# One inference step of a gated recurrent layer: the FFN's fourth input pair as seven block products, and a moved split, cast and key page in branch A

## The chip, the core and the metric

The kernel runs on one core of a Trainium2 chip. The metric is the device time of the whole program in microseconds (us), here the median of three runs. Engines are called as the profile calls them: PE is TensorE, DVE VectorE, ACT ScalarE, POOL GpSimd, SP SyncE, which only issues DMAs here.

## What is computed

One layer of a decoder on 520 tokens (512 of a prompt, 8 of a sample group), with D = 1024 and an inner FFN width of 2816. The arithmetic that the change touches, cut from the reference:

```python
z = h @ w_in                                 # xr, gr, q, k, v, fl, ga, gb are columns of z
xc, conv_new = causal_dwconv(xr, conv_buf, conv_w, conv_b)
hr, h_last = rg_lru(xc, h0, pos0, rg_wr, rg_br, rg_wi, rg_bi, rg_lambda)
ya = (hr * gelu(gr)) @ w_proj_a              # branch A
yb = attend(q, k, v, logf).reshape(B, T, ATTN_W) @ w_proj_b
mixed = (sigmoid(ga) * ya + sigmoid(gb) * yb) @ w_o
x = x + g1 * mixed
h2 = rms_norm(x, norm2_g) * (1.0 + sc2) + sh2
gu, up = split(h2 @ w_ffn_in, 2)
x = x + g2 * ((silu(gu) * up) @ w_ffn_out)
```

The sample group's attention also runs over its cache: 64 pages of keys and 64 of values, 512 KB each.

## The kernel before

**Products.** Everything is kept with features on the partitions and the 520 tokens on the free axis, in two halves of 260 (`L_` and `R_` in the FFN). Each operand of a large product is held as a rounded part and the rest (names ending in h and l for activations, `whi` and `wlo` for weights, both halves of `wb` for a block), and each product of a 128x128 weight block with 260 tokens is three matmuls: rounded by rounded, rest of the weight by rounded, rounded by rest of the activation. `product` makes a 128-feature output: eight k blocks by three matmuls by two halves, 48 matmuls into two PSUM banks. Products are counted by `state["n"]`. Numbers 0 to 31 are the input projections of branch A and the gates (xr, gr, ga, gb), 32 is k0, 33 v0, 34 to 41 are pa0 to pa7, the products with `w_proj_a`; then come the rest of attention, pb, wo and the FFN.

**Weights.** SP fetches chunks of 1024x256 (`wraw`, two buffers; chunks of w_fo go into the pool of page buffers `pg`). `split_upto(n)` makes every unit up to number n ready: ScalarE casts (`whi`, line 250), VectorE subtracts (`wlo`, line 252). A chunk's buffer comes free when its last unit is split. `split` does the same for activations (lines 346 and 347).

**Branch A.** `lru_gates` makes the recurrence's gates by small matmuls and sigmoids, then `lru_exp`, `lru_root`, `lru_scan`; `lru_mul` multiplies the state by the gelu, and `lru_g` splits that into the operand `g` of the pa products (`gh`, `gl`). In the last round of the loop (i = 6) the order is written out: behind the gates of 6, with `issue_after`, come `both(lru_mul, 4)`, `both(lru_g, 4)` and the split of the weights of two products ahead; then ga6, the gates of 7, ga7. A ga product's two banks are evacuated by ScalarE (`tA`, line 1194).

**Cache pages.** At each of the products 0 to 41 `tick` fetches as many pages of keys as the table `KEYS` says, from GpSimd's queue, multiplies them with the queries on VectorE and sums; `VALUES` names the products that also fetch pages of values. Small matmuls `pv` take these up.

**FFN.** The inner width is 22 pairs of 128 (gate and up). Pairs 0 and 1 (`PLAIN`) are made together, the left half of the tokens first, while the right half of h2 is still being normalised (banks fi0 to fi3). Pairs 2 and 3 (below `GROUP`) are two plain products each, `fig` and `fiu`. From pair 4 on `fast_tile` makes a pair with seven block products in Strassen's manner (Winograd's form) instead of eight: the two 128-feature outputs and the two k halves are the 2x2 blocks of the weights, the two k halves and the two token halves those of the input. The products A11, S2, S3, S1, A12, A22, S4 have four k blocks each, 12 matmuls, and go into the banks X, Y, W, Z (fi4x, fi4y and so on). Names are those of the weight's block: A11, A12 and A22 are blocks of it, S1 to S4 sums that GpSimd makes in `split_block` (`ws`, line 265). The input's sums are `u` and `w` (four tiles each, one of each for k and k + 4), which `h2_blocks` makes once on GpSimd, four instructions of 128x260 for each k, and which `split_blocks` splits into `tuh`, `tul`, `twh`, `twl`. S2 and S3 take w's halves; S1 and A22 take u's; A11, A12 and S4 take h2 itself. `JOIN` puts two products of the FFN's second matrix (`fo`) behind S2 and A12 of a pair.

**What sets the order.** Tile's scheduler orders the instructions on each engine from their order in the code, a simulated run and the priorities; `issue_after` adds an order and no data. `defer(k, fn)` runs fn at the end of the k-th product from now. `h2_blocks` stands before pair 2 in the code, and `split_blocks` behind the first and the second of the next products.

Of the kernel before, what the change touches and what calls it, by code (L numbers as in the profile page):

```python
# [67 lines left out]
def kernel(ctx, tc, xT, par1, par, gates, b_f, cst, cse, own, cache_k, cache_v, cache_lf, pt,  # L68
# [75 lines left out]
    GROUP = 4  # L144
    PLAIN = 2
    LAST = 16
    JOIN = {}
# [15 lines left out]
    for jt in range(FF // 128):  # L163
        c = len(chunks)
        chunks.append(cols(w_fi, 128 * jt, 128) + cols(w_fi, FF + 128 * jt, 128))
        if jt < GROUP:
            whole(c)
            continue
        for name in BLOCKS:
            units.append((c, name, 4))  # L170
            if name in JOIN[jt]:
                g, i = JOIN[jt][name]
                if i % 2 == 0:
                    joined.add(len(chunks))
                    chunks.append(cols(w_fo, 128 * i, 256, 128 * GROUP * g, GROUP))
                units.append((max(joined), 128 * (i % 2), GROUP))
# [17 lines left out]
    def flush():  # L194
        while stores:
# [4 lines left out]
    KEYS = dict(zip(range(42), (2, 2, 0, 0, 1, 2, 2, 2, 1, 1, 1, 1, 2, 2, 2, 1, 0, 1, 0, 1, 2, 2, 2, 2, 1, 1, 1, 1, 2, 2, 1, 2,  # L200
                                1, 1, 1, 2, 1, 1, 1, 1, 2, 0)))
    VALUES = (19, 21, 22, 25, 28, 29, 31, 35, 37, 39)
# [56 lines left out]
    def split_block(raw, name):  # L259
        if name == "A11":  # L260
# [3 lines left out]
            blocks.update(A11=a11, A12=a12, A22=a22, S1=s1, S2=s2, S3=s3, S4=s4)  # L264
            pool.tensor_tensor(s1, a21, a22, ALU.add)  # L265
            pool.tensor_tensor(s2, s1, a11, ALU.subtract)
            pool.tensor_tensor(s3, a11, a21, ALU.subtract)
            pool.tensor_tensor(s4, a12, s2, ALU.subtract)
# [325 lines left out]
    m = None  # L594
# [606 lines left out]
    for i in range(0, KT, 2):  # L1201
# [35 lines left out]
        else:  # L1237
            lru_gates(i)
            with tc.issue_after(state["gate"].ins):
                both(lru_mul, i - 2)  # L1240
                both(lru_g, i - 2)
                split_upto(state["n"] + 2)
            gate_a(i)
            lru_gates(i + 1)
            gate_a(i + 1)
# [516 lines left out]
    L_, R_ = slice(0, HALF), slice(HALF, NT)  # L1762
    tb, traw = [], {}

    def h2_blocks(k):
        b1, b2 = h2raw[k], h2raw[k + 4]
        u, w = slot("u"), slot("w")
        with tc.issue_after(state["blocks"].ins) if k != 3 else nullcontext():
            first = pool.tensor_tensor(w[:, R_], b2[:, R_], b1[:, R_], ALU.subtract)
        if k == 3:  # L1770
            state["blocks"] = first
        with tc.issue_after(state["blocks"].ins):
            pool.tensor_tensor(u[:, L_], b1[:, R_], b1[:, L_], ALU.subtract)
            pool.tensor_tensor(w[:, L_], b2[:, R_], u[:, L_], ALU.subtract)
            pool.tensor_tensor(u[:, R_], b2[:, L_], w[:, L_], ALU.subtract)
        traw[k] = u, w

    def split_blocks(k0):
        with tc.issue_after(state["silu"].ins):
            for k in range(k0, k0 + 2):  # L1780
                u, w = traw[k]
                tb.append((split("tu", u), split("tw", w)))

# [5 lines left out]
    def fast_tile(jt, ac):  # L1789
# [9 lines left out]
        for m_, name in enumerate(BLOCKS):  # L1799
# [24 lines left out]
            run_later(n)  # L1824
            if name in JOIN[jt]:
                g, i = JOIN[jt][name]
# [5 lines left out]
    for j in range(2):  # L1832
        for m in range(2 * PLAIN):
# [7 lines left out]
            if j or m:  # L1841
                with tc.issue_after(state["root"].ins):
                    for fn, *args in ready:
                        fn(*args)
                ready.clear()
            first = u + 2 * PLAIN
            if j == 0:
                load_chunks(units[first + m][0])
            elif m:
                split_upto(first + m - 1)  # L1850
    for t in ts:
# [3 lines left out]
    for jt in range(PLAIN, FF // 128):  # L1855
        if jt == PLAIN:
            for k in (3, 0, 1, 2):
                h2_blocks(k)
            defer(0, lambda: split_blocks(0))
            defer(1, lambda: split_blocks(2))  # L1860
        ac.append(fast_tile(jt, ac) if jt >= GROUP else ffn_tile(jt))
    last_product(ac[LAST:])

# [63 lines left out]
```

## Time and profile before

| | before |
|---|---|
| median of 3 runs | 1000.09 us |
| lowest, highest | 999.8, 1001.43 us |
| profiled execution, its span | 1000.87 us, 999.1 us |
| instructions | 21582 |
| TensorE (PE) | 8156 matmuls |
| VectorE (DVE) | 774.9 us busy, 1386 instructions |
| ScalarE (ACT) | 553.1 us busy, 1131 instructions |
| GpSimd (POOL) | 357.9 us busy, 444 instructions |
| DMA | 204.03 MB, 204 GB/s over the span |

The span runs from the first to the last instruction that is counted as work; the time of the execution lies 1.77 us above it. Rows of a timeline give the start and the duration of an instruction in us from the start of the span, its engine, line, operation, output and inputs with shapes, and in square brackets how long the engine had stood idle and what released it. SPq and POOLq are queues of DMA issues. Rows of waits give the idle time of one group of instructions in all, its count, and the longest. Rows of windows give the stretch and its length, and for each engine the busy time and the count (PE, PEld, DVE, ACT, POOL), then the granted clock, the DMA share and the rate in GB/s.

### The profile page before, as it was taken

What the parts mean: (1) busy time and instruction counts of PE and PEld (TensorE: products, weight loads), DVE (VectorE), ACT (ScalarE), POOL (GpSimd) and SP (SyncE); (2) the same over time, 40 slices, a digit from 0 to 9 for tenths busy, and PEclk for the clock granted to TensorE, in tenths of its full rate; (3) what the DMA queues carried; (4) which work ended last, traced back from release to release, by engine and by line L of the source; (5) the groups of instructions that cost most, each with busy time, mean ns of one, the idle gap of its engine ahead of it and who ended that gap; (6) DMA issues with size and microseconds to landing.
All of it is one profiled execution on the core that took longest, in us unless ns stands there. A gap on an engine that the chain in (4) does not pass through costs nothing.

```text
span 999.1 us, 21582 instructions
## 1 busy us (share of the span) xinstructions
PE 981.7 (98%) x8156; PEld 912.6 (91%) x8156; DVE 774.9 (78%) x1386; ACT 553.1 (55%) x1131; POOL 357.9 (36%) x444
## 2 busy tenths in 40 slices
PE   7999999999999999999999999999999999999996
PEld 5889999999898988888888879999999999999996
DVE  5599899979899877876664445879888887888764
ACT  5435669766941576777762224544444444445453
POOL 0254142523354166545300003394334242434112
PEclk9999999999999999999999999999999999999998
DMA  9989756887979998897778994142424334133112
GB/s 320 335 282 325 224 169 185 262 288 243 307 235 365 324 287 274 286 294 200 256 265 290 341 338 130 45 127 64 128 64 127 97 94 121 49 106 107 64 64 86
DMA packets 164506, 204.03 MB, mean 204 GB/s; under 512 B 9635, under 2 KB 128051, under 8 KB 164339
## 3 DMA queue, kind: packets, MB, share of 16 engines
q1 hardware_dynamic: 148162, 151.14, 47.9%
q0 software_dynamic: 12560, 45.10, 13.6%
q10 hardware_dynamic: 3680, 6.42, 1.7%
q8 instruction: 64, 1.05, 0.5%
q14 instruction: 40, 0.32, 0.1%
HBM read 189.54 MB, written 13.09 MB: 203 GB/s over the span
## 4 chain that ended last, share of the span: by engine, by line
PE 87%; ACT 4%; DVE 4%; DMA 2%; issue 1%; SPq 0%; POOL 0%; POOLq 0%; DVEq 0%; ACTq 0%
PE fo L311 13%; PE wo L311 5%; PE pb L311 4%; PE gb L311 4%; PE v L311 4%; PE k L311 4%; PE ga L311 3%; PE xr L311 3%; PE pa L311 3%; PE pv L946 3%; PE gr L311 2%; PE po L1416 2%; PE sc L1353 2%; PE ptt L1382 2%; PE ada L378 2%; PE fi L311 1%
## 5 line engine op out<-in xcount | busy, mean ns | idle before, releaser
L250 ACT CAST whi<-wraw 128x1024 fp32r<-128x1024 f32 (+1 forms) x79 | 82.1, 1040 | 92.2 <-PE pb L311 34.3
L252 DVE TENSOR_TENSOR wlo<-wraw,whi 128x1024 fp32r<-128x1024 f32 (+1 forms) x79 | 97.8, 1238 | 24.4 <-ACT whi L250 22.3
L274 ACT CAST wb<-ws 128x512 fp32r<-128x512 f32 x72 | 44.8, 622 | 88.4 <-PE fo L311 61.2
L311 PE MATMUL fo<-ach,wb 128*128 128x260 f32 x512 | 93.4, 283 | 0.0
L275 DVE TENSOR_TENSOR wb<-wraw,wb 128x512 fp32r<-128x512 f32 x86 | 76.0, 883 | 5.3 <-ACT wb L274 4.3
L311 PEld LDWEIGHTS fo<-ach,wb 128*128 128x128 f32 x512 | 78.9, 188 | 0.0
L265 POOL TENSOR_TENSOR ws<-wraw 128x512 f32<-128x512 f32 x18 | 24.4, 1355 | 151.8 <-DMA wraw<-in_w_fi_dram 86.3
L274 ACT CAST wb<-wraw 128x512 fp32r<-128x512 f32 x86 | 53.5, 622 | 35.8 <-ACT cp L1814 6.2
L311 PE MATMUL fo<-acl,wb 128*128 128x260 f32 x256 | 72.3, 282 | 0.0
L275 DVE TENSOR_TENSOR wb<-ws,wb 128x512 fp32r<-128x512 f32 x72 | 60.8, 845 | 14.2 <-ACT wb L274 12.5
L794 POOL DMA_DIRECT2D pg<-in_cache_k_dram x70 | 37.7, 539 | 92.0 <-DVE S L858 47.3
L857 DVE TENSOR_TENSOR pg<-pg,qb 128x1024 f32<-128x1024 f32 x48 | 57.9, 1220 | 2.2 <-DMA pg<-in_cache_k_dram 2.1
L858 DVE TENSOR_REDUCE S<-pg 128x16 f32<-128x1024 f32 x48 | 57.3, 1208 | 0.3
L1373 POOL TENSOR_SCALAR p<-p,mu 128x128 f32<-128x128 f32 (+3 forms) x28 | 34.5, 1243 | 53.8 <-DVE mu L1369 40.5
L311 PEld LDWEIGHTS fo<-acl,wb 128*128 128x128 f32 x256 | 48.3, 189 | 0.0
L1367 ACT ACTIVATE p<-p,mu 128x128 f32<-128x128 f32 (+3 forms) x64 | 35.4, 555 | 17.3 <-DVE mu L1366 16.8
L407 POOL TENSOR_TENSOR ss<-ss,sq 128x260 f32<-128x260 f32 x10 | 7.8, 784 | 84.8 <-ACT sq L406 84.6
L311 PE MATMUL ga<-hh,whi 128*128 128x260 f32 x128 | 36.7, 286 | 1.3 <-ACT tA L1194 1.3
L311 PE MATMUL v<-hh,whi 128*128 128x260 f32 x128 | 37.6, 294 | 0.0
L311 PE MATMUL k<-hh,whi 128*128 128x260 f32 x128 | 37.5, 293 | 0.0
L311 PE MATMUL pb<-oh,whi 128*128 128x260 f32 x128 | 37.2, 290 | 0.2 <-ACT oh L1474 0.2
L311 PE MATMUL gb<-hh,whi 128*128 128x260 f32 x128 | 37.3, 291 | 0.0
(1122 smaller groups left out, 3967.2 us busy)
## 6 DMA issues: line engine op xcount, KB each, us to landing
wraw<-in_w_fi_dram SPq DMA_DIRECT2D x44, 512.0 KB, 4.9
pg<-in_cache_k_dram POOLq DMA_DIRECT2D x42, 512.0 KB, 5.6
pg<-in_cache_v_dram SPq DMA_DIRECT2D x42, 512.0 KB, 5.3
araw<-in_ada_w_dram SPq DMA_DIRECT2D x38, 512.0 KB, 8.0
wraw<-in_w_in_dram SPq DMA_DIRECT2D x28, 512.0 KB, 6.7
wraw<-in_w_in_dram SPq DMA_DIRECT2D x11, 1024.0 KB, 9.4
pg<-in_cache_v_dram POOLq DMA_DIRECT2D x22, 512.0 KB, 5.7
wraw<-in_w_fo_dram SPq DMA_DIRECT2D x16, 512.0 KB, 5.7
```

The lines of the kernel that those rows point to most:

```text
L250: state["act"] = act.copy(hi[:, :k1 - k0], src)
L252: state["last"] = dve.tensor_tensor(lo[:, :k1 - k0], src, hi[:, :k1 - k0].bitcast(F32), ALU.subtract)
L265: pool.tensor_tensor(s1, a21, a22, ALU.add)
L274: state["act"] = act.copy(t[:, :4], src)
L275: state["last"] = dve.tensor_tensor(t[:, 4:], src, t[:, :4].bitcast(F32), ALU.subtract)
L311: state["mm"] = pe.matmul(out[:, :t1 - t0], lhsT=wt[k], rhs=at, start=k == 0 and m == 0, stop=k == nk - 1 and m == 2)
L794: done.append(eng.dma_start(pg, cache[bass.ds(r, 1), :, c0:c1].rearrange("a p c -> (a p) c")))
L857: dve.tensor_tensor(pg, pg, q, ALU.mult)
L858: last = dve.tensor_reduce(S[r // 2][:, c:c + H], pg.rearrange("p (h d) -> p h d", d=DH), AX.X, ALU.add)
L946: pe.matmul(pv[0][32 * gq:32 * gq + 32, :], lhsT=pw[r][:, c:c + 32], rhs=pgs[gq // 2][:, 512 * hf:512 * hf + 512], start=j == 0, stop=j == ...
L1367: act.activation(p[:, :n + 128], p[:, :n + 128], AF.Exp, bias=mu[:, 0:1], scale=-1.0, accum_out=mu[:, 1:2])
L1373: (pool.tensor_scalar(p, p, mu[:, 2:3], None, ALU.mult) if a and i + 1 < KT else act.activation(p, p, AF.Copy, scale=mu[:, 2:3]))
```

## The change

There are two parts. In the FFN pair 3 becomes a block product too (`FAST` = 3), without `fo` products in it. The input's block sums are needed one pair earlier: `h2_blocks` is called while pairs 0 and 1 are still computed, the sums for k = 0 and 2 are made by VectorE and those for 1 and 3 by GpSimd, the splits for 0 and 2 come right ahead of pair 2, those for 1 and 3 behind its first product, and w is split ahead of u. GpSimd's sums of the weights S1 and S3 wait in order for its last input sum, and one unit of weights less is split in the last step of pairs 0 and 1. In branch A, the last round splits one g and one weight unit where it split two of each, and the second g comes behind ga6. In `KEYS`, pa0 loses its page and pa2 takes it.

```diff
@@ -143,6 +143,7 @@
         chunks.append(cols(w_o, 128 * i))
     GROUP = 4
     PLAIN = 2
+    FAST = 3
     LAST = 16
     JOIN = {}
     for jt in range(GROUP, LAST):
@@ -163,12 +164,12 @@
     for jt in range(FF // 128):
         c = len(chunks)
         chunks.append(cols(w_fi, 128 * jt, 128) + cols(w_fi, FF + 128 * jt, 128))
-        if jt < GROUP:
+        if jt < FAST:
             whole(c)
             continue
         for name in BLOCKS:
             units.append((c, name, 4))
-            if name in JOIN[jt]:
+            if name in JOIN.get(jt, ()):
                 g, i = JOIN[jt][name]
                 if i % 2 == 0:
                     joined.add(len(chunks))
@@ -198,7 +199,7 @@
     later = {}
 
     KEYS = dict(zip(range(42), (2, 2, 0, 0, 1, 2, 2, 2, 1, 1, 1, 1, 2, 2, 2, 1, 0, 1, 0, 1, 2, 2, 2, 2, 1, 1, 1, 1, 2, 2, 1, 2,
-                                1, 1, 1, 2, 1, 1, 1, 1, 2, 0)))
+                                1, 1, 0, 2, 2, 1, 1, 1, 2, 0)))
     VALUES = (19, 21, 22, 25, 28, 29, 31, 35, 37, 39)
     LAST_POOL = 41
 
@@ -262,9 +263,11 @@
             s12, s34 = (pgp.tile([128, 8, 128], F32, name="ws", tag="pg") for _ in range(2))
             s1, s2, s3, s4 = s12[:, :4], s12[:, 4:], s34[:, :4], s34[:, 4:]
             blocks.update(A11=a11, A12=a12, A22=a22, S1=s1, S2=s2, S3=s3, S4=s4)
-            pool.tensor_tensor(s1, a21, a22, ALU.add)
+            with tc.issue_after(state["h2"].ins):
+                pool.tensor_tensor(s1, a21, a22, ALU.add)
             pool.tensor_tensor(s2, s1, a11, ALU.subtract)
-            pool.tensor_tensor(s3, a11, a21, ALU.subtract)
+            with tc.issue_after(state["h2"].ins):
+                pool.tensor_tensor(s3, a11, a21, ALU.subtract)
             pool.tensor_tensor(s4, a12, s2, ALU.subtract)
         return split_four(blocks[name])
 
@@ -1238,9 +1241,10 @@
             lru_gates(i)
             with tc.issue_after(state["gate"].ins):
                 both(lru_mul, i - 2)
-                both(lru_g, i - 2)
-                split_upto(state["n"] + 2)
+                lru_g(i - 2)
+                split_upto(state["n"] + 1)
             gate_a(i)
+            lru_g(i - 1)
             lru_gates(i + 1)
             gate_a(i + 1)
             both(lru_exp, i)
@@ -1760,26 +1764,30 @@
 
 
     L_, R_ = slice(0, HALF), slice(HALF, NT)
-    tb, traw = [], {}
+    tb, traw = {}, {}
 
     def h2_blocks(k):
         b1, b2 = h2raw[k], h2raw[k + 4]
         u, w = slot("u"), slot("w")
+        eng = dve if k in (0, 2) else pool
         with tc.issue_after(state["blocks"].ins) if k != 3 else nullcontext():
-            first = pool.tensor_tensor(w[:, R_], b2[:, R_], b1[:, R_], ALU.subtract)
+            first = eng.tensor_tensor(w[:, R_], b2[:, R_], b1[:, R_], ALU.subtract)
         if k == 3:
             state["blocks"] = first
         with tc.issue_after(state["blocks"].ins):
-            pool.tensor_tensor(u[:, L_], b1[:, R_], b1[:, L_], ALU.subtract)
-            pool.tensor_tensor(w[:, L_], b2[:, R_], u[:, L_], ALU.subtract)
-            pool.tensor_tensor(u[:, R_], b2[:, L_], w[:, L_], ALU.subtract)
+            eng.tensor_tensor(u[:, L_], b1[:, R_], b1[:, L_], ALU.subtract)
+            eng.tensor_tensor(w[:, L_], b2[:, R_], u[:, L_], ALU.subtract)
+            end = eng.tensor_tensor(u[:, R_], b2[:, L_], w[:, L_], ALU.subtract)
+        if eng is pool:
+            state["h2"] = end
         traw[k] = u, w
 
-    def split_blocks(k0):
+    def split_blocks(*ks):
         with tc.issue_after(state["silu"].ins):
-            for k in range(k0, k0 + 2):
-                u, w = traw[k]
-                tb.append((split("tu", u), split("tw", w)))
+            for k in ks:
+                u, w = traw.pop(k)
+                sw_ = split("tw", w)
+                tb[k] = split("tu", u), sw_
 
     def h2_block(name, k):
         pair, part = {"A11": (h2[k], L_), "A12": (h2[k + 4], L_), "S4": (h2[k + 4], R_), "S1": (tb[k][0], L_),
@@ -1822,7 +1830,7 @@
                 act.activation(sw[:, R_], Z, AF.Silu)
                 close(Y, R_)
             run_later(n)
-            if name in JOIN[jt]:
+            if name in JOIN.get(jt, ()):
                 g, i = JOIN[jt][name]
                 product(f"fo{g}_{i}", ac[GROUP * g:GROUP * g + GROUP], lambda j, b_, i=i: residual(i, b_, 5, j))
         return out
@@ -1843,22 +1851,23 @@
                     for fn, *args in ready:
                         fn(*args)
                 ready.clear()
+            if j and m == 1:
+                for k in (3, 0, 1, 2):
+                    h2_blocks(k)
             first = u + 2 * PLAIN
             if j == 0:
                 load_chunks(units[first + m][0])
             elif m:
-                split_upto(first + m - 1)
+                split_upto(first + min(m - 1, 1))
     for t in ts:
         out = pair_out()
         split_part(out, t)
         ac.append(out)
     for jt in range(PLAIN, FF // 128):
         if jt == PLAIN:
-            for k in (3, 0, 1, 2):
-                h2_blocks(k)
-            defer(0, lambda: split_blocks(0))
-            defer(1, lambda: split_blocks(2))
-        ac.append(fast_tile(jt, ac) if jt >= GROUP else ffn_tile(jt))
+            split_blocks(0, 2)
+            defer(0, lambda: split_blocks(1, 3))
+        ac.append(fast_tile(jt, ac) if jt >= FAST else ffn_tile(jt))
     last_product(ac[LAST:])
 
 
```

**VectorE, end of h2 and pairs 0 and 1.** These are the rows from the last rest of h2 on (`h2l`) in the kernel before, `wlo` being rests of weights, `sw` the product of gate and up parts, `acl` the rest of that product. The number at the end of a name is that of the tile.

```order
L1629 TENSOR_TENSOR h2l_9478<-h2r_9472,h2h_9477 128x260
L252 TENSOR_TENSOR wlo_9950<-wraw_9760,whi_9949 128x1024
L1675 TENSOR_TENSOR sw_9733<-fi1_1_9923,sw_9733 128x260
L252 TENSOR_TENSOR wlo_9980<-wraw_9760,whi_9979 128x1024
L1634 TENSOR_TENSOR acl_10014<-sw_9733,ach_10013 128x520
L252 TENSOR_TENSOR wlo_10010<-wraw_9868,whi_10009 128x1024
L1675 TENSOR_TENSOR sw_9734<-fi3_1_9983,sw_9734 128x260
L1634 TENSOR_TENSOR acl_10018<-sw_9734,ach_10017 128x520
L347 TENSOR_TENSOR tul_10106<-u_10027,tuh_10105 128x520
L252 TENSOR_TENSOR wlo_10122<-wraw_9868,whi_10121 128x1024
L347 TENSOR_TENSOR twl_10110<-w_10028,twh_10109 128x520
```

In the changed kernel the same place reads (h2r are the raw tiles of h2, u and w their sums):

```order
L1633 TENSOR_TENSOR h2l_9478<-h2r_9472,h2h_9477 128x260
L1774 TENSOR_TENSOR w_9956<-h2r_9459,h2r_9433 128x260
L1778 TENSOR_TENSOR u_9955<-h2r_9433 128x260
L1779 TENSOR_TENSOR w_9956<-h2r_9459,u_9955 128x260
L1774 TENSOR_TENSOR w_9968<-h2r_9472,h2r_9446 128x260
L1780 TENSOR_TENSOR u_9955<-h2r_9459,w_9956 128x260
L1778 TENSOR_TENSOR u_9967<-h2r_9446 128x260
L253 TENSOR_TENSOR wlo_9974<-wraw_9760,whi_9973 128x1024
L1679 TENSOR_TENSOR sw_9733<-fi1_1_9923,sw_9733 128x260
L1779 TENSOR_TENSOR w_9968<-h2r_9472,u_9967 128x260
L253 TENSOR_TENSOR wlo_10004<-wraw_9760,whi_10003 128x1024
L1780 TENSOR_TENSOR u_9967<-h2r_9472,w_9968 128x260
```

Eight sums of the input stand between `h2l` and `acl`, and the two rests of `wraw_9868`, pair 3's chunk, have gone, since it is now taken in blocks; the tul and twl come later. Behind these rows follow one `acl` and the rests of two weight blocks, `wb_10072` of S2 and `wb_10069` of A11.

**VectorE, the first input sums that a block product takes.** Before, they are for pair 4 and stand beside pair 3's products (`fiu3`):

```order
L347 TENSOR_TENSOR tul_10182<-u_10039,tuh_10181 128x520
L275 TENSOR_TENSOR wb_10212<-ws_10203,wb_10212 128x512
L1634 TENSOR_TENSOR acl_10047<-sw_10045,ach_10046 128x260
L347 TENSOR_TENSOR twl_10186<-w_10040,twh_10185 128x520
L275 TENSOR_TENSOR wb_10209<-wraw_10048,wb_10209 128x512
L347 TENSOR_TENSOR tul_10190<-u_10021,tuh_10189 128x520
L347 TENSOR_TENSOR twl_10194<-w_10022,twh_10193 128x520
L275 TENSOR_TENSOR wb_10270<-ws_10204,wb_10270 128x512
L275 TENSOR_TENSOR wb_10215<-wraw_10051,wb_10215 128x512
L1675 TENSOR_TENSOR sw_10197<-fiu3_0_10279,sw_10197 128x260
L1634 TENSOR_TENSOR acl_10199<-sw_10197,ach_10198 128x260
L1675 TENSOR_TENSOR sw_10197<-fiu3_1_10307,sw_10197 128x260
```

Changed, they are for pair 3, beside pair 2's (`fiu2`); fi3_1 is the bank of the second up product of pairs 0 and 1, right half:

```order
L1679 TENSOR_TENSOR sw_9734<-fi3_1_10007,sw_9734 128x260
L1638 TENSOR_TENSOR acl_10038<-sw_9734,ach_10037 128x520
L350 TENSOR_TENSOR twl_10042<-w_9956,twh_10041 128x520
L350 TENSOR_TENSOR tul_10046<-u_9955,tuh_10045 128x520
L350 TENSOR_TENSOR twl_10050<-w_9968,twh_10049 128x520
L350 TENSOR_TENSOR tul_10054<-u_9967,tuh_10053 128x520
L278 TENSOR_TENSOR wb_10078<-ws_10063,wb_10078 128x512
L278 TENSOR_TENSOR wb_10075<-ws_10064,wb_10075 128x512
L350 TENSOR_TENSOR twl_10134<-w_9962,twh_10133 128x520
L350 TENSOR_TENSOR tul_10138<-u_9961,tuh_10137 128x520
L1679 TENSOR_TENSOR sw_10057<-fiu2_0_10169,sw_10057 128x260
L350 TENSOR_TENSOR twl_10142<-w_9950,twh_10141 128x520
```

The `twl` come ahead of the `tul`, and the rows run through from `acl` to the last `twl` (10142, of the fourth k) with one product from PSUM in between, where before the rests of pair 3's weights and its first products stood among them. Line 275 has become 278, 347 is now 350.

**ScalarE, at ga6 and ga7.** Before, from the last gate of 6 on (`gh` is a rounded g, `whi` a rounded weight, `tA` a half of the ga product):

```order
L1136 ACTIVATE gate_3915<-gate6_1_1_3930,prm_77 64x260
L346 CAST gh_3944<-ge_3644 128x520
L250 CAST whi_3954<-wraw_3772 128x1024
L346 CAST gh_3949<-ge_3837 128x520
L250 CAST whi_4150<-wraw_3772 128x1024
L1194 ACTIVATE tA_3958<-ga6_0_4014 128x260
L1194 ACTIVATE tA_3958<-ga6_1_4040 128x260
```

Changed, with the names as before:

```order
L1139 ACTIVATE gate_3915<-gate6_1_1_3930,prm_77 64x260
L349 CAST gh_3944<-ge_3644 128x520
L251 CAST whi_4150<-wraw_3772 128x1024
L1197 ACTIVATE tA_3949<-ga6_0_4009 128x260
L1197 ACTIVATE tA_3949<-ga6_1_4035 128x260
L349 CAST gh_4061<-ge_3837 128x520
```

One cast of weights has moved ahead (it now stands in front of `xch_3907`, ahead of the gates), and the second `gh` behind the two evacuations of ga6.

## The prediction

> **What bounds the kernel now.** I read the page's busy shares and its chain first, then TensorE's own waits, then the busy time stage by stage, and last the timelines of the two places that the change touches.
>
> ```profile
> PE 981.7 (98%) x8156; PEld 912.6 (91%) x8156; DVE 774.9 (78%) x1386; ACT 553.1 (55%) x1131; POOL 357.9 (36%) x444
> PE 87%; ACT 4%; DVE 4%; DMA 2%; issue 1%; SPq 0%; POOL 0%; POOLq 0%; DVEq 0%; ACTq 0%
> PE ga L311 <- ACT tA L1194: 1.3, 1, 1.3
> PE pv L946 <- DMA pg<-in_cache_v_dram: 0.3, 1, 0.3
> 700.00:950.00 250.00, 250.00 (x2087) 250.00 (x2086) 205.20 (x392) 117.92 (x241) 90.74 (x60) 1.00 0.34 96
> ```
>
> TensorE is busy for 98% of the span and carries 87% of the chain. Between 20 us and the last ten, the two waits shown are its longest that this change can reach, and through the FFN (700 to 950 us) it has no gap at all at a granted clock of 1.00. So a matmul that goes away there is worth its full time, and any wait that is put in front of TensorE costs its full time. The sum needs three terms of gain and one of loss.
>
> **Fewer matmuls.** The fourth pair (jt=3) is now four products of 24 matmuls each, two of the gate and two of the up part.
>
> ```profile
> 657.25 5.75 PE fig L311 x48
> 663.00 5.74 PE fiu L311 x48
> 668.74 5.74 PE fig L311 x48
> 674.48 5.74 PE fiu L311 x48
> ```
>
> These are pieces of the chain: start, length, count. The first two are pair jt=2, which stays, the last two pair jt=3: 11.48 us for 96 matmuls, 0.1196 us each. Seven block products of 4 x 3 matmuls are 84, so twelve go: 12 x 0.1196 = **-1.43 us**, from 668.74 on.
>
> **The moved split.** In branch A, product ga7 waits.
>
> ```profile
> 249.19 0.63 ACT L346 CAST xch<-xc 128x520 fp32r<-128x520 f32 x1 [1.59 <-DVE xc L1113]
> 255.09 0.63 ACT L346 CAST gh<-ge 128x520 fp32r<-128x520 f32 x1
> 255.62 1.04 ACT L250 CAST whi<-wraw 128x1024 fp32r<-128x1024 f32 x1
> 256.57 0.62 ACT L346 CAST gh<-ge 128x520 fp32r<-128x520 f32 x1
> 257.10 1.04 ACT L250 CAST whi<-wraw 128x1024 fp32r<-128x1024 f32 x1
> 258.16 0.67 ACT L1194 ACTIVATE tA<-ga 128x260 f32<-128x260 f32 x2
> 256.19 1.07 PE L946 MATMUL pv<-pg,pw 128*32 128x512 f32 x8
> 258.60 0.39 PE L311 MATMUL ga<-hh,whi 128*128 128x260 f32 x1 [1.34 <-ACT tA L1194]
> 239.15 0.39 SPq L214 DMA_DIRECT2D wraw<-in_w_in_dram  x1
> DMA to landing us min/median/max: 8.7/9.0/9.4
> ```
>
> TensorE is done with pv at 257.26, but ga7's bank is free only once ScalarE has evacuated ga6 (tA, 258.16), which stands behind two casts of activations and two of weights. In the new order one weight cast goes ahead of xch and one cast of activations behind tA, so tA moves up by 0.53 + 0.95 = 1.48 us (the distances of the rows' starts) to about 256.7 and the 1.34 us go. What is late next: the cast that moved ahead of xch needs its chunk, issued at 239.15 and, at 8.7 to 9.4 us to landing, there at 247.9 to 248.6. The cast then ends at 248.9 to 249.6, against 249.19 for xch, so ScalarE slips by 0 to 0.4 us and ga7 by no more than 0.3. The other instructions of the swap stay beside matmuls; VectorE gets a key page's multiply ahead of its wait for gh, where it stood idle. I take **-1.3 us**; ends 0 (something else frees the bank as late) and -1.4.
>
> **The key page.** One page fewer is fetched at product pa0 and one more at pa2, so the two value pages ahead of them leave GpSimd's queue earlier by one issue and find one 512 KB transfer less in front.
>
> ```profile
> 308.99 1.05 PE L946 MATMUL pv<-pg,pw 128*32 128x512 f32 x4 [0.26 <-DMA pg<-in_cache_v_dram]
> 300.83 0.53 POOL L794 DMA_DIRECT2D pg<-in_cache_k_dram  x1
> 338.07 0.43 DVE L1198 TENSOR_TENSOR tA<-pa,tA 128x260 f32<-128x260 f32 x1 [0.55 <-PE pa L311]
> ```
>
> The wait of 0.26 us for the value page should go: one issue is 0.53 us. The page's two VectorE instructions move into the products where VectorE already waits for TensorE (last row). I take **-0.2 us**, between -0.3 and +0.5.
>
> **The new wait.** Block products need the input's block sums (u, w), their split (tuh, tul, twh, twl) and the weights' block sums (ws) one pair earlier, 11.5 us sooner. TensorE reaches product A11 at 668.74 and S2 at 670.18, and needs S2's twl of the fourth k at 671.26. What VectorE has to do before that is fixed by its queue as shown in the section on the change, from the last h2l to the last twl. How long that takes depends on one thing which the trace shows well:
>
> ```profile
> 648.34 0.43 DVE L1629 TENSOR_TENSOR h2l<-h2r,h2h 128x260 fp32r<-128x260 f32 x1
> 650.61 1.26 DVE L252 TENSOR_TENSOR wlo<-wraw,whi 128x1024 fp32r<-128x1024 f32 x1 [1.84 <-ACT whi L250]
> 652.61 1.67 DVE L252 TENSOR_TENSOR wlo<-wraw,whi 128x1024 fp32r<-128x1024 f32 x1 [0.39 <-ACT whi L250]
> 653.15 1.72 POOL L1775 TENSOR_TENSOR u<-h2r,w 128x260 f32<-128x260 f32 x1
> 658.41 0.74 POOL L1773 TENSOR_TENSOR u<-h2r 128x260 f32<-128x260 f32 x1
> 663.08 1.30 POOL L265 TENSOR_TENSOR ws<-wraw 128x512 f32<-128x512 f32 x1
> 671.69 0.42 DVE L1634 TENSOR_TENSOR acl<-sw,ach 128x260 fp32r<-128x260 f32 x1
> 672.03 0.42 DVE L1675 TENSOR_TENSOR sw<-fiu,sw 128x260 f32<-128x260 f32 x1
> 672.36 0.68 DVE L347 TENSOR_TENSOR tul<-u,tuh 128x520 fp32r<-128x520 f32 x1
> 672.97 1.80 DVE L275 TENSOR_TENSOR wb<-ws,wb 128x512 fp32r<-128x512 f32 x1
> 672.43 1.79 POOL L265 TENSOR_TENSOR ws<-wraw 128x512 f32<-128x512 f32 x1 [1.23 <-DMA wraw<-in_w_fi_dram]
> 666.66 0.99 SPq L214 DMA_DIRECT2D wraw<-in_w_fi_dram  x2
> 680.15 0.69 DVE L347 TENSOR_TENSOR twl<-w,twh 128x520 fp32r<-128x520 f32 x1
> ```
>
> A VectorE instruction with both operands in SBUF never runs beside a GpSimd instruction: each waits until the other has ended. The weight rest of 652.61 runs until 654.28, and GpSimd's sum of 653.15, 0.74 alone, ends 0.6 after that, at 654.87. The ws sum of 672.43 (1.30 alone) starts behind the tul that ends at 673.04, and the wb of 672.97 waits for it: 1.80 where the tul before it took 0.68. So when both have work they take turns, and every GpSimd instruction adds its time to VectorE's queue: about 0.6 us for one of 128x260, 1.12 (1.80 - 0.68) for one of 128x512.
>
> The count starts at 648.77, where h2l ends. VectorE's own part, by the distance of consecutive starts: eight block sums at 0.34 (671.69 to 672.03) are 2.7; two weight rests at 1.18 (1.26 less the overlap of 0.08) 2.4; two acl and seven tul or twl at 0.61 (672.36 to 672.97) 5.5; four wb at 0.6 2.4; three products from PSUM at 0.34 1.0. Together 14.0 us. GpSimd's part: its eight block sums at 0.6 (4.8), four ws sums of jt=3 and four of jt=4 at 1.12 (9.0), together 13.8, of which some 0.9 lie beside the PSUM products and the queue's few gaps. The jt=4 sums come in time to be in the way: their chunk is fetched once jt=2's second weight rest is done, which the taking of turns puts at 659.3, and a chunk is 5.8 us from issue to its first sum (666.66 to 672.43): 665.1. So the last twl is done near 648.8 + 14.0 + 12.9 = 675.7. Following the three queues with the wait of each instruction, where turns and casts fall as they do, I get 674.8 for the twl of the second k and 676.4 for that of the fourth. The same count made for the kernel before gives 681.0 for its last twl; the row of 680.15 ends at 680.84.
>
> TensorE thus waits 674.8 - 670.5 = 4.3 us after S2's first k and 0.8 again before its fourth: **+5.2 us** with the issue. After it, weights and tul are ready in time (jt=3's last weight blocks at 679.8 and earlier, TensorE past A12 at 681.1), and from jt=4 on nothing differs. The ends: 0, if the two engines do not hold each other up in the new order; 6.5, if each GpSimd sum costs its 1.30 and not 1.12. I take 5.2, since the same counting meets the trace of before within 0.2 us.
>
> This trace has the row of 672.97 with the longer time, and the Trainium skill, page "Trainium Architecture — The Big Picture", section "What this means for kernel authors", says that what VectorE and GpSimd share is an exclusive lock and not a split of bandwidth. By that rule the sum is the one made here; by a split of bandwidth, with both merely slower, the VectorE queue would end soon enough and the gain alone would be left. By that rule, the trace agrees (1.80 against 0.68 us).
>
> **The sum.** -1.43 - 1.3 - 0.2 + 5.2 = **+2.3 us**. The span of 999.1 becomes 1001.4, the profiled run of 1000.87 (1.77 around its span) becomes 1003.2. That run lies 0.78 above the median of the three runs, 1000.09, so for the median I forecast 1002.4.
>
> **The rivals.** *No wait (faster).* VectorE gets through its 14.0 us with few turns given away, and the last twl is there before 671.26. That needs no more than 8.5 us of GpSimd's 13.8 in between. For it: half of the block sums leave GpSimd, which shortens its queue by 8 x 0.7. Against it: each of the rows above shows the hold. It gives 1000.09 - 2.9 = 997.2. The point at which it decides is 671.26.
>
> *Half a wait.* The chunk of jt=4 lands later than 665.1, and two or more of its four sums fall behind the last twl; each takes 1.12 off. Two of them leave 3.0 us of wait: 1000.2. For it: the transfer is near in time to the fo chunk's. Against it: 5.8 us are seen for jt=5's chunk under the same traffic.
>
> *The clock drops.*
>
> ```profile
> 256.00:260.00 4.00, 2.66 (x21) 1.71 (x22) 3.75 (x5) 3.93 (x8) 1.06 (x2) 1.00 0.99 299
> 990.00:992.00 2.00, 1.13 (x8) 1.05 (x8) 0.64 (x3) 0.76 (x3) 0.00 (x0) 0.90 0.00 0
> 992.00:994.00 2.00, 0.33 (x2) 0.04 (x1) 1.64 (x6) 0.00 (x0) 0.00 (x0) 0.50 0.00 0
> ```
>
> An idle time of 1.34 us left the granted clock at 1.00 (first row); at the tail, with TensorE half idle, it fell to 0.50 within some four microseconds. A wait of 4.3 us lies beyond the first and near the second. If it falls, one or two block products (1.44 us each) run at half speed: +1.4 to +2.9, I take 2: 1004.4. The Trainium skill, page "TensorE: Matmul & The Clock Gate", section "Part 1: The HAM clock gate (the "warmup" mystery)", has one free-running window of about 3.4 us both for losing and for regaining the full clock; by it a wait of 4.3 us holds a whole idle window about one time in four, and the estimate from that page is a loss of 1.7 us.
>
> **How the numbers follow.** The forecast, 1001.0 to 1003.8, has 0.44; the clock rival 0.23; half a wait 0.19; no wait 0.14. A run can tell this kernel from no change from about 0.2% on, which is 2.0 us: 998.1 and 1002.1. Slower then takes a little over half of the forecast and all of the clock rival, 0.47; the same takes the rest of the forecast and most of half a wait, 0.37; faster takes no wait and the low end of half a wait, 0.16. The range goes from 998.0, which leaves out no wait, to 1005.4, with the upper end of the clock rival.
>
> **What would show it.** In the profile of the changed kernel TensorE has a wait at the second block product of fi3 (fi3y) of some 5 us, released by VectorE's twl, and the four twl end near 669, 672, 675 and 676. The wait of ga7 for tA is gone, and the wait of pv at the products pa too. The time of the seven fi3 products without waits is 10.0 us. If VectorE's block sums of 128x260 take 0.4 each while GpSimd is busy, the taking of turns is wrong and so is the sign. If ga7 still waits, another releaser stands behind tA. If the clock of the stretch from 675 to 680 is below 1.00, the clock rival holds.

## The result, and the profile after

The changed kernel takes 1003.88 us (median of six runs, 1003.55 to 1006.59), the kernel before 1000.28 beside it (six runs, 999.8 to 1001.43): ratio 1.0038, 95% interval 1.0027 to 1.0048. It is slower by 3.6 us. The profiled execution took 1003.96 us, with a span of 1002.2.

The page's busy shares and its chain, after:

```profile
PE 981.4 (98%) x8144; PEld 912.9 (91%) x8144; DVE 787.0 (79%) x1403; ACT 554.5 (55%) x1138; POOL 349.9 (35%) x440
PE 89%; ACT 3%; DVE 2%; DMA 2%; issue 1%; POOL 1%; SPq 0%; DVEq 0%; ACTq 0%; POOLq 0%
```

Twelve matmuls are gone (8156 to 8144), and yet TensorE is busy for the same 981 us: some of the others have become slower. Its waits, of those that the change can reach (what waits for what, us in all, times, longest):

```profile
PE fi3y L1813 <- DVE twl L350: 3.4, 1, 3.4
...
PE ga L314 <- ACT tA L1197: 0.6, 1, 0.6
```

The forecast wait stands where it was put, at S2 of pair 3, released by VectorE's twl. The stretch around it, in steps of 2 us:

```profile
668.00:670.00 2.00, 1.73 (x15) 1.51 (x13) 2.00 (x2) 2.00 (x4) 1.92 (x2) 1.00 0.00 0
670.00:672.00 2.00, 0.00 (x0) 0.00 (x0) 2.00 (x4) 0.02 (x1) 0.05 (x1) 0.90 0.00 0
672.00:674.00 2.00, 0.91 (x4) 0.91 (x5) 2.00 (x5) 0.00 (x0) 0.00 (x0) 0.50 0.00 0
674.00:676.00 2.00, 2.00 (x10) 1.81 (x10) 2.00 (x5) 1.53 (x4) 0.00 (x0) 0.50 0.00 0
676.00:678.00 2.00, 2.00 (x11) 2.00 (x11) 2.00 (x5) 1.69 (x5) 0.00 (x0) 0.50 0.00 0
678.00:680.00 2.00, 2.00 (x17) 2.00 (x16) 1.90 (x5) 0.94 (x2) 0.00 (x0) 0.89 0.77 217
```

The granted clock falls to 0.50 while TensorE waits and stays there for 6.8 us (the last 0.4 of the row of 670, the three rows behind it, and the first 0.4 of the row of 678). 5.4 of these come after the twl is there, at 673.05. What that costs stands in the chain of the end (start, length, count):

```profile
668.91 1.70 DVE twl L350
670.61 0.61 DVE tul L350
671.22 1.20 DVE wb L278 x2
672.43 0.62 DVE twl L350
673.05 0.04 issue
673.09 2.14 PE fi3y L1813 x7
675.23 2.60 PE fi3w L1813 x12
677.83 1.76 PE fi3z L1813 x12
679.59 1.43 PE fi3x L1813 x12
```

At half the clock twelve matmuls take 2.60 us where they take 1.43 a few rows on. The turns of VectorE and GpSimd, from the timelines of both:

```profile
647.18 0.43 DVE L1633 TENSOR_TENSOR h2l<-h2r,h2h 128x260 fp32r<-128x260 f32 x1
...
648.42 0.97 DVE L1778 TENSOR_TENSOR u<-h2r 128x260 f32<-128x260 f32 x1
...
665.39 1.79 DVE L350 TENSOR_TENSOR twl<-w,twh 128x520 fp32r<-128x520 f32 x1
667.11 1.80 DVE L350 TENSOR_TENSOR tul<-u,tuh 128x520 fp32r<-128x520 f32 x1
668.84 1.78 DVE L350 TENSOR_TENSOR twl<-w,twh 128x520 fp32r<-128x520 f32 x1
670.54 0.69 DVE L350 TENSOR_TENSOR tul<-u,tuh 128x520 fp32r<-128x520 f32 x1
...
672.35 0.69 DVE L350 TENSOR_TENSOR twl<-w,twh 128x520 fp32r<-128x520 f32 x1
...
673.91 0.68 DVE L350 TENSOR_TENSOR twl<-w,twh 128x520 fp32r<-128x520 f32 x1
...
664.87 1.76 POOL L270 TENSOR_TENSOR ws<-wraw 128x512 f32<-128x512 f32 x1
666.59 1.77 POOL L268 TENSOR_TENSOR ws<-ws,wraw 128x512 f32<-128x512 f32 x1
668.43 1.62 POOL L271 TENSOR_TENSOR ws<-wraw,ws 128x512 f32<-128x512 f32 x1
```

As long as GpSimd has sums to make, the same split takes 1.8 us on VectorE; with GpSimd done it takes 0.69. The ends show turns, and not two engines that are merely slower: GpSimd's sums end at 666.63, 668.36 and 670.05, and VectorE's splits 0.55 to 0.57 behind each of them, at 667.18, 668.91 and 670.62. The block sums of the input show it too: they take up to 0.97 us beside GpSimd's, where the prediction named 0.4 as the sign that it was wrong.

To see in which stretch time goes, the starts of the same matmuls in two traces are compared. The table gives how much longer each stretch took than in the kernel before (a minus is a gain): from xr7 to ga7 (the moved split), from ga7 to the last pa product (the key pages), and from the first FFN products to pair 5's first. It also has all runs that follow, with medians beside that of the kernel before from the same chip. The kernel before differs from chip to chip (1000.28 to 1001.2), so two kernels are compared by their ratios to it, not by their medians.

| kernel | to ga7 | to pa7 | FFN to pair 5 | median | before | ratio (95%) |
|---|---|---|---|---|---|---|
| the change | -0.07 | -1.31 | +4.95 | 1003.88 | 1000.28 | 1.0038 (1.0027-1.0048) |
| ffn_only | 0.00 | +1.57 | +5.21 | 1006.4 | 1001.2 | 1.0052 (1.0039-1.0066) |
| branch_only | -1.17 | -0.88 | +0.16 | 999.76 | 1001.2 | 0.9986 (0.9977-0.9995) |
| keys_only | 0.00 | -1.45 | -0.19 | 999.34 | 1000.97 | 0.9985 (0.9976-0.9994) |
| cast_late | -1.41 | -0.69 | +4.56 | 1003.95 | 1001.2 | 1.0032 (1.0020-1.0044) |
| sums_late | -1.02 | -1.26 | +6.39 | 1006.13 | 1001.2 | 1.0049 (1.0035-1.0063) |
| sums_last | -1.41 | -1.10 | +4.79 | 1004.14 | 1000.97 | 1.0033 (1.0021-1.0045) |
| sums_last2 | -0.67 | -1.30 | +2.17 | 1001.47 | 1001.13 | 1.0007 (0.9998-1.0016) |
| sums_dve | -1.42 | -1.13 | +4.70 | 1003.1 | 1000.97 | 1.0021 (1.0012-1.0030) |
| best | -1.42 | -0.06 | +2.73 | 1001.6 | 1001.13 | 0.9999 (0.9990-1.0008) |
| best2 | -0.95 | -1.29 | -0.24 | 998.38 | 1001.08 | 0.9975 (0.9964-0.9985) |

Between the pa products and the FFN the kernels that come out of pa earlier give back 0.2 to 0.4 us; no single wait shows for it, and it is left open.

### The profile page after: what moved, and what is told of

The parts are those of the page before. It is cut to its first block, busy times and chain, and to the rows that moved or that the text cites. A ratio compares the mean times of both kernels' runs of the same rounds, so it can differ in the third digit from the quotient of the medians.

```text
span 1002.2 us, 21578 instructions
## 1 busy us (share of the span) xinstructions
PE 981.4 (98%) x8144; PEld 912.9 (91%) x8144; DVE 787.0 (79%) x1403; ACT 554.5 (55%) x1138; POOL 349.9 (35%) x440
## 3 DMA queue, kind: packets, MB, share of 16 engines
q8 instruction: 64, 1.05, 0.5%
## 4 chain that ended last, share of the span: by engine, by line
PE 89%; ACT 3%; DVE 2%; DMA 2%; issue 1%; POOL 1%; SPq 0%; DVEq 0%; ACTq 0%; POOLq 0%
PE fo L314 13%; PE v L314 5%; PE wo L314 5%; PE k L314 5%; PE pa L314 5%; PE pb L314 4%; PE gb L314 4%; PE ga L314 4%; PE gr L314 3%; PE xr L314 3%; PE pv L949 3%; PE po L1420 2%; PE sc L1357 2%; PE ptt L1386 2%; PE ada L381 2%; PE qc L580 1%
## 5 line engine op out<-in xcount | busy, mean ns | idle before, releaser
L251 ACT CAST whi<-wraw 128x1024 fp32r<-128x1024 f32 (+1 forms) x77 | 79.9, 1040 | 89.1 <-PE pb L314 34.5
L277 ACT CAST wb<-ws 128x512 fp32r<-128x512 f32 x76 | 47.2, 622 | 95.8 <-PE fo L314 61.6
L278 DVE TENSOR_TENSOR wb<-ws,wb 128x512 fp32r<-128x512 f32 x76 | 66.4, 875 | 14.2 <-ACT wb L277 12.3
```

Source lines behind the costliest of these rows:

```text
L251: state["act"] = act.copy(hi[:, :k1 - k0], src)
L277: state["act"] = act.copy(t[:, :4], src)
L278: state["last"] = dve.tensor_tensor(t[:, 4:], src, t[:, :4].bitcast(F32), ALU.subtract)
```

## The experiments

**The parts alone.** *ffn_only* is the change without its edits in branch A and in `KEYS`, *branch_only* these alone, *keys_only* the table alone:

```diff
-                                1, 1, 1, 2, 1, 1, 1, 1, 2, 0)))
+                                1, 1, 0, 2, 2, 1, 1, 1, 2, 0)))
```

> The FFN part of the change alone; branch A and the key pages as before. If the two parts add up: TensorE waits 3.4 us at fi3y for twl, the granted clock falls to 0.66 for ten microseconds, 1.4 us of matmuls go, and the time is 4.9 us above the kernel before (about 1005.2). If instead the early part of the change shifts what meets at fi3y (a chunk or an h2 half that is late), the time is below 1004 or above 1006.

> Branch A's part and the key pages alone; the FFN as before. If the parts add up: the matmuls of pa end 1.3 to 1.4 us earlier, almost all of it from the value page's wait at pv and only 0.1 from ga7, and the time is 1.0 to 1.4 us below the kernel before (about 999.1). Rival: what is gained here is lost again in attention, where another wait is due: no difference.

> The kernel before with the new table of key pages alone. If the value page's wait at pv is what branch A's part gained beside ga7: the eight matmuls of pv run as one group of 1.0 us, pa is 0.9 to 1.3 us earlier behind it, ga7 keeps its 1.3 us, and the time is 0.9 to 1.3 us below the kernel before. If that gain comes from the moved cast: no difference.

The medians add up: +5.2 and -1.4 make +3.8, where the change has +3.6. Branch A's part is a gain and the FFN's part alone the loss, +4.95 to +5.21 us in both kernels that have it. keys_only keeps its wait of 1.3 us at ga7 and is still 1.6 us faster, so the table alone brings what branch A's part brings. What the moved split adds is seen in the traces (1.17 us to ga7 in branch_only), but not in the medians: the intervals of branch_only and keys_only lie almost on each other. Where the table helps is seen at the pv matmuls near 308 us, behind pa2, in the timelines of before, of keys_only and of ffn_only:

```profile
308.99 1.05 PE L946 MATMUL pv<-pg,pw 128*32 128x512 f32 x4 [0.26 <-DMA pg<-in_cache_v_dram]
```

```profile
308.07 1.06 PE L946 MATMUL pv<-pg,pw 128*32 128x512 f32 x8
```

```profile
310.21 1.05 PE L949 MATMUL pv<-pg,pw 128*32 128x512 f32 x4 [1.80 <-DMA pg<-in_cache_v_dram]
311.41 1.05 PE L949 MATMUL pv<-pg,pw 128*32 128x512 f32 x4
```

With both pages there, eight matmuls take 1.06 us together; when the second page is late, each group of four takes 1.05 by itself. Before, the four that were ready began at 307.67 and the next product at 309.97, 2.3 us for what takes 1.0 in the change. A wait shown as 0.26 cost 1.3 us. With the old table it varies from profile to profile (0.26 in before, 1.80 in ffn_only). With the new one it is mostly gone, but not always: the eight take 1.48 us in branch_only and 1.61 in best, and there too a value page is what the wait is put down to (0.3 and 0.4 us). That is why these two gain less up to pa7 in the table.

**GpSimd's sums held back (sums_late).** A copy of one column of the last twl on GpSimd, ahead of its sums for pair 4, holds them until that twl is written. VectorE's queue is the same, row by row.

```diff
+            state["fast"] = state.get("fast", 0) + 1
+            if state["fast"] == 2:
+                state["h2"] = pool.tensor_copy(small("gd", 128, 1, 1), tb[3][1][1][:, :1].bitcast(F32))
```

> The changed kernel, with GpSimd's four weight sums of pair 4 held until the last twl of pair 3 is written; VectorE's queue is the same, instruction by instruction. If taking turns with GpSimd makes the wait: the twl, tul and acl from 664 us on take 0.61 instead of 1.7, the last twl is done near 670.5, the wait at fi3y is below 0.3 us, the granted clock stays at 1.00, and the time is 6.0 us lower than the change's, about 997.8. If VectorE's own queue is too long: the wait stays above 2 us and the time above 1002. If the sums are then late for pair 4: a new wait at fi4y, 1 to 3 us.

The wait at fi3y falls from 3.4 to 0.4 us, and the splits are as short as alone, but the kernel is 4.9 us slower than before, where the change is 3.6, and the granted clock falls to 0.50 again, for 3.4 us. Waits, and VectorE's and GpSimd's timeline:

```profile
PE fi4x L1816 <- DVE wb L281: 2.3, 1, 2.3
PE fi3z L1816 <- DVE fi3z L1804: 1.3, 1, 1.3
PE fi3x L1816 <- DVE wb L281: 1.1, 1, 1.1
...
PE fi3y L1816 <- DVE twl L353: 0.4, 1, 0.4
```

```profile
665.11 0.69 DVE L353 TENSOR_TENSOR twl<-w,twh 128x520 fp32r<-128x520 f32 x1
...
672.21 3.30 DVE L281 TENSOR_TENSOR wb<-wraw,wb 128x512 fp32r<-128x512 f32 x2
...
673.24 1.73 POOL L273 TENSOR_TENSOR ws<-wraw 128x512 f32<-128x512 f32 x1
```

So the turns do make the wait at fi3y: without GpSimd, VectorE's queue is in time to 0.4 us. But the sums moved only to where the weight blocks of A12, A22 and S4 are due, and these pay: two wb take 3.30 where they took 1.28 in the change.

**Further back (sums_last, sums_last2).** Now the copy reads pair 3's last weight block, GpSimd's order is S1, S2, S3, S4, and pair 4's S2 is split later on VectorE; sums_last2 keeps ScalarE's cast of it behind the copy of fi3z too (the diff shows it with that). Both also make the weights ready six us ahead during pair 3, by `state["lead"]`, where the change has eleven.

```diff
-                state["h2"] = pool.tensor_copy(small("gd", 128, 1, 1), tb[3][1][1][:, :1].bitcast(F32))
+                state["h2"] = pool.tensor_copy(small("gd", 128, 1, 1), state["s4"][0].bitcast(F32))
...
-        return split_four(blocks[name])
+        late = state["fast"] == 2 and name == "S2"
+        with tc.issue_after(state["y"].ins) if late else nullcontext():
+            with tc.issue_after(state["cp"].ins) if late else nullcontext():
+                return split_four(blocks[name])
```

> The changed kernel, with GpSimd's four weight sums of pair 4 held until VectorE has written the last weight block of pair 3 (S4), in the order S1, S2, S3, S4, and pair 4's S2 block split behind pair 3's sums from PSUM. If the two engines' turns are all that TensorE waited for in pair 3: waits there are 0.5 us in all, the granted clock stays at 1.00, pair 3 brings 1.4 us less 0.5, and the time is 5.5 to 6.2 us below the change's and 2.0 to 2.8 below the kernel before. If pair 4 pays instead: a wait of 1 to 3 us at fi4y or fi4w, and the time lies between the two. If VectorE is too slow by itself: waits of over 1 us inside pair 3 with GpSimd idle beside it.

> As the kernel before it (GpSimd's sums of pair 4 behind VectorE's last weight block of pair 3), but ScalarE too makes the cast of pair 4's S2 behind its copy of fi3z. If ScalarE's queue was what brought the 3.9 us back (its cast waited for the sum, and the copy of fi3z stood behind the cast): the copy starts near 674, the waits in pair 3 are 0.4 to 0.8 us in all, the granted clock stays at 1.00, and TensorE is 6 us earlier at fi4y than in the change; the time is 997.5 to 998.5 where the kernel before is 1000.3 to 1001. If the sums are then too late for pair 4: a wait of up to 2 us at fi4y.

sums_last has one long wait of 3.9 us in place of those (and 0.4 at fi3y), and the clock falls with it; ScalarE's timeline and the wait:

```profile
676.89 0.62 ACT L281 CAST wb<-ws 128x512 fp32r<-128x512 f32 x1 [3.83 <-POOL ws L271]
677.42 0.37 ACT L1827 COPY cp<-fi3z 128x260 f32<-128x260 f32 x1
...
PE fi3w L1818 <- DVE fi3y L1806: 3.9, 1, 3.9
```

ScalarE stood for 3.83 us before a cast that wanted the held sum, with the copy of fi3z, which TensorE needed, right behind. That was my own knot, and sums_last2 undoes it: the clock stays at 1.00, and 2.6 of the 4.8 us are back. It is level with the kernel before. What remains is spread: waits of 0.4 at fi3y, 0.7 at fi3w, and 0.4 and 0.8 at the fo products of pair 4, which want an acl that stands behind weight blocks of 1.4 to 1.8 us, beside GpSimd's sums of pair 5.

**All input sums on VectorE (sums_dve).** GpSimd's sums of the weights, which waited in order for its last input sum, now wait for its last instruction of h2 instead.

```diff
-        eng = dve if k in (0, 2) else pool
+        eng = dve
```

> The changed kernel, with all sixteen block sums of the input on VectorE (eight more), none on GpSimd. If every instruction of either engine takes its time from one shared turn (0.56 us for a sum on GpSimd, 0.34 on VectorE): the twl end 8 x 0.22 = 1.8 us earlier, the wait at fi3y falls from 3.4 to about 1.6, and with a shorter halved stretch the time is 2 to 4.5 us below the change's. If VectorE's own queue is what is too long: it gets 8 x 0.34 = 2.7 longer, the wait grows to 6 us, and the time is 2.5 us above the change's or more.

There is no wait at fi3y, but TensorE comes there 5 us late. The time is lost ahead of it, since GpSimd, with no input sums to make and held back no longer than that, starts the weights' sums of pair 3 among the h2l of the right half (at 644.45 us; in the change at 655.22):

```profile
PE fi L314 <- DVE h2l L1633: 2.4, 2, 1.9
```

Neither theory had this; it is the same turns in a third place, and half the clock once more. The price of a sum on either engine isn't measured by it, as GpSimd's later sums moved too.

**The moved cast (cast_late).** Here gr6's cast and the second g come behind the evacuation of ga6.

```diff
+            lead, state["lead"] = state["lead"], 6
             gate_a(i)
-            lru_g(i - 1)
+            state["lead"] = lead
+            with tc.issue_after(state["tA"].ins):
+                split_upto(state["n"] + 1)
+                lru_g(i - 1)
```

> The changed kernel, with the cast of gr6's weights and the second g behind the evacuation of ga6 instead of ahead of xch. If the cast's wait for its chunk is what ate the gain at ga7: tA starts near 255.7 instead of 257.9, the wait of ga7 (0.55) and that of the gates (0.33) are gone, and TensorE is 1.2 us earlier at gr6, about 1002.7 in all. Rival: another thing holds ga7 or gr6 then (gr6's weights, cast later): within 0.3 us of the change.

tA starts at 256.02, ga7 has no wait, and 1.41 us are gained there. But the weights are then late in the pa products, and about half goes back:

```profile
256.02 0.67 ACT L1199 ACTIVATE tA<-ga 128x260 f32<-128x260 f32 x2
...
PE pa L314 <- DVE wlo L253: 0.6, 1, 0.6
```

It is 2.75 us slower than the kernel before on its chip, where the change is 3.6, and the intervals of the two ratios overlap: no gain is shown in the whole.

**Everything together (best, best2).** best has all input sums on VectorE, GpSimd's sums of pair 3 behind the last h2l (by a copy of one of its columns), those of pair 4 as in sums_last2, and cast_late. best2 drops cast_late and puts the rest of fig2's weights behind the first four input sums:

```diff
+                h2_blocks(3)
+                split_upto(first)
+                with tc.issue_after(state["last"].ins):
+                    for k in (0, 1, 2):
+                        h2_blocks(k)
```

> All findings together: the input's sixteen block sums on VectorE, GpSimd's sums of pair 3 behind the last h2l and those of pair 4 behind pair 3's last weight block, ScalarE's and VectorE's S2 of pair 4 behind pair 3's sums, and the cast of gr6 behind the evacuation of ga6. If the turns have been counted rightly: no wait of over 0.4 us from 640 to 700 us, ga7 without its wait, and a time 3 to 4 us below the kernel before, about 997. If sixteen sums make VectorE late for the splits: a wait at fi3y of 0.5 to 2 us.

> As the kernel before it, but the rest of fig2's weights stands behind the first four of the input's sums on VectorE instead of behind fifteen, and branch A's cast of gr6 is where the change has it. If the 2.4 us at fig2 were only the place of that rest in VectorE's queue: no wait of over 0.4 us from 640 to 700 us, granted clock 1.00 there, pair 3 brings its 1.4 us, TensorE is at fi4y 1.3 to 1.5 us more ahead than at pair 2, and the time is 2.5 to 3.5 us below the kernel before (about 998). Rival: VectorE, with 5.4 us of sums more than before in this stretch, is late in another place (fiu2's weights or fi3y) by 0.5 to 2 us: 999 to 1001.

best has one wait of 2.4 us, at pair 2, whose weights' rest stands behind fifteen sums, and the clock falls with it; behind that, pair 3 runs through without a wait. Its gain in branch A is nearly gone as well, by the late value page (0.6 us) and by a wait of 0.6 us in pa, as in cast_late.

```profile
PE fig L321 <- DVE wlo L253: 2.4, 1, 2.4
656.00:658.00 2.00, 0.25 (x3) 0.04 (x1) 2.00 (x6) 1.09 (x3) 0.00 (x0) 1.00 0.00 0
658.00:660.00 2.00, 1.32 (x6) 1.32 (x7) 2.00 (x3) 0.00 (x0) 0.00 (x0) 0.59 0.00 0
```

best2 has lost that wait too. Its stretches of 10 us and its only wait there:

```profile
660.00:670.00 10.00, 10.00 (x85) 10.00 (x84) 10.00 (x19) 8.76 (x19) 0.00 (x0) 1.00 0.38 103
670.00:680.00 10.00, 10.00 (x85) 9.95 (x84) 7.90 (x12) 3.69 (x9) 8.61 (x7) 1.00 0.72 211
680.00:690.00 10.00, 9.52 (x77) 9.11 (x77) 10.00 (x20) 5.91 (x13) 4.40 (x3) 1.00 0.28 79
...
PE fo L321 <- DVE acl L1645: 0.5, 1, 0.5
```

GpSimd does nothing from 660 to 670, while VectorE makes the splits. From the second product of pair 2 (fiu2) to S2 of pair 4 best2 gains 1.26 us and best 1.31, close to the 1.43 of twelve matmuls; in best2 the stretch from there to pair 5, with the fo products of pair 4, takes 1.0 of it back. best2 is faster than the kernel before, 998.38 against 1001.08, ratio 0.9975 (0.9964 to 0.9985). Most of that comes from branch A, though: 0.95 to ga7 and 1.29 to pa7, against 0.24 in the FFN. That it is faster than the new table alone (keys_only, 0.9985) isn't shown, since the intervals overlap.

## Why the prediction was right, and where its terms were wrong

The time lies in the range and on the side that was likeliest, 1.5 us above the forecast. The mechanism of the loss was right, and the place and the releaser of the wait. The sizes of three terms were off, and the clock, which the sum left out, was the largest error: in the profiled runs the split misses by +1.2, the key page by -1.1, the wait by -1.7 and the clock by +2.9. That these add up to so little is luck.

- *Fewer matmuls, -1.43*: right. It shows by itself only in kernels without a wait in pair 3 (-1.26 in best2, -1.31 in best).
- *The moved split, -1.3*: right in mechanism, wrong in what I took to be late next. The profiled execution gained 0.07. I had the cast that moves ahead of xch slip by 0 to 0.4 us; its chunk landed later than the 8.7 to 9.4 us from issue which the trace of before showed (9.4 is that of this very chunk):

```profile
249.48 1.05 ACT L251 CAST whi<-wraw 128x1024 fp32r<-128x1024 f32 x1 [2.05 <-DMA wraw<-in_w_in_dram]
250.43 0.62 ACT L349 CAST xch<-xc 128x520 fp32r<-128x520 f32 x1
...
257.92 0.67 ACT L1197 ACTIVATE tA<-ga 128x260 f32<-128x260 f32 x2
...
238.98 0.39 SPq L215 DMA_DIRECT2D wraw<-in_w_in_dram  x1
```

  The cast starts 10.5 us after the issue, xch 1.24 late, and tA gets 0.24 of the 1.48 us. Six other kernels with the same code gain more, and the gain falls as the landing gets later: 1.41 and 1.42 us where the chunk is there 8.8 and 9.0 us after its issue, 1.17 at 9.3, 0.95 and 1.02 at 9.5, 0.67 at 9.8, and 0.07 at 10.4, in the change. So the term is right on a good landing and near zero on a bad one, and ga7 still waits for tA, behind the late cast. cast_late, without that cast ahead of xch, has the gain in full.
- *The key page, -0.2*: mis-sized by the largest factor. I took the wait's own 0.26 us; it was worth 1.3 in the profile of before, since the wait splits a group of matmuls that otherwise run beside each other.
- *The new wait, +5.2*: right in place and releaser, 3.4 in size. The count of turns was good: the twl of the second k and the fourth end 25.4 and 27.0 us after the last h2l (673.03 and 674.59, from 647.61) where I had 26.0 and 27.6. TensorE wanted the first of them at 669.56, 0.2 us later after h2l than I took, and the second wait of 0.8 was swallowed by the halved clock.
- *The clock*: a rival with a chance of 0.23, and it was what happened. In the change it costs 2.9 us: from the start of fiu2 to S2 of pair 4 the trace has 23.6 us, of which 17.2 are work at full clock (48, 84 and 12 matmuls at 0.1196) and 3.5 the wait with its issue (669.56 to 673.09). I priced it at 2.0 and gave it too small a chance, from a wait of 1.34 us that left the clock alone and from the tail.

In the Trainium skill, page "TensorE: Matmul & The Clock Gate", section "Part 1: The HAM clock gate (the "warmup" mystery)", the array returns to half speed after an idle window of about 3.4 us, free-running. The lengths agree with the trace: the halved stretches here last 3.4 us in sums_late and cast_late and 6.8, twice that, in the change. The condition, read as a fully idle window, does not: in best a single wait of 2.4 us was enough, in sums_dve one of 1.9 us, and in the 3.4 us ahead of the fall TensorE had been busy for 1.5 us in the change, 1.4 in sums_late, 1.3 in best and 1.5 in sums_dve. By that reading I had made it one time in four; every kernel here with a wait of 1.9 us or more in the FFN had the fall. The pv wait of 1.80 us in ffn_only did not: counted in steps of 3.41 us back from that kernel's fall in the FFN, the step around it (306.8 to 310.3 us) has 1.6 us of work. In sums_late the step before the last (675.5 to 678.9) has 1.7 and left the clock alone too. So in these stretches the line lies near 1.5 us of work in a step. It isn't the whole rule: at the tail of before, among matmuls of other shapes, the clock fell with 2.3 us of work in the step.

So the change is 4.95 us in the FFN (-1.43 + 3.5 + 2.9), less about 1.4 in branch A. Other stretches, one longer and others shorter, bring that to the 3.1 us between the two profiled runs, where the medians have 3.6; these are not explained. That turns with GpSimd make the wait is shown by sums_late. That they make the loss is shown by sums_last2 and best2, in which more than half of it and all of it go; these change the order and the place of the sums and of the splits of weights near them, and how early weights are made ready in pair 3, which wasn't changed by itself. What is open: why the same chunk is there 8.8 us after its issue in one execution and 10.4 in another.

## What to carry to other kernels

Where two engines take turns, count their work as one queue, over the whole stretch up to the next slack: holding back one engine's part moved the loss from the splits to the weights, then to another engine's queue, before there was a place for it. A wait of TensorE can cost more than its length: it may split a group that ran side by side (1.3 us for 0.26), and the waits of 1.9 us and more in the FFN here brought the clock down, which in the change cost 2.9 us on top of 3.5. And an instruction that moves ahead of a queue's critical one must have its data for certain, not by the median landing.

## What the runs showed of the hardware

- VectorE and GpSimd alternate instruction by instruction where VectorE reads two SBUF operands: 128x520 splits of 0.69 us take 1.8 beside sums of 128x512. With one of VectorE's operands in PSUM they do not: in best fi3w<-fi3w,u takes 0.42 in the middle of a sum of 1.63.
- Eight pv matmuls, which write four strips of 32 partitions, take 1.06 us together, and the four that belong to one page take 1.05.
- The granted clock falls and returns in steps of 3.4 us, and in sums_dve a wait of 1.9 us started a fall. In the change, in sums_late, in sums_dve and in best TensorE had been busy for 1.3 to 1.5 us of the 3.4 before; 1.6 and 1.7 left the clock at 1.00.
